# A decoder layer on one core: the second block of each gate/up pair comes only by adding transfers, and the next pair's first product moves ahead of product 7

## The chip, the core and the metric

The kernel runs on one core of a Trainium2 chip. TensorE (PE) multiplies, VectorE (DVE) and ScalarE (ACT) work on tiles, GpSimd (POOL) and SyncE (SP) here mainly start transfers. The metric is the device time of one execution in microseconds, as the median of several runs. A profile shows one further execution in detail.

## The reference, cut to what matters

```python
def _swiglu(x, w_gate, w_up, w_down):
    return (jax.nn.silu(x @ w_gate) * (x @ w_up)) @ w_down
...
h = _layer_norm(ALPHA * h + 0.5 * _swiglu(h, ffn1_w_gate[l], ffn1_w_up[l], ffn1_w_down[l]), ln1_g[l], ln1_b[l])
mix = _mixer(h, positions, w_in[l], ...)          # two attention branches, gates, output projection
h = _layer_norm(ALPHA * h + mix, ln2_g[l], ln2_b[l])
h = _layer_norm(ALPHA * h + 0.5 * _swiglu(h, ffn2_w_gate[l], ffn2_w_up[l], ffn2_w_down[l]), ln3_g[l], ln3_b[l])
```

There are 256 rows of 2048 values, the hidden width of each FFN is 5632, and everything is float32. The change touches the two products with `w_gate` and `w_up` of both FFNs, called the gate/up stage.

## The kernel before

**Products in float32.** A weight tile of 128x1024 (two k-tiles of 128 rows by 512 columns) is read from memory as it is ("raw", "sraw") and split into a high part, cast by ACT (`split`, L154), and the remainder, which DVE computes (L155). Both go into a ring of six slot pairs, "wring". One product of a tile then takes three matmuls (`triple`, L208 to L210: high by high, low by high, high by low).

**Gate/up.** Its columns form 22 chunks of 512 columns, gate and up interleaved. `project` does the first two in the ordinary way. The other 20 go as ten pairs through `Hybrid.group`. A pair has 16 k-tiles of each of two chunks. Of these, k-tiles 0 to 3 and 4 to 7 of the first chunk and of the second form four blocks of weights, "11", "21" (first chunk) and "12", "22" (second), each of two tiles, s0 and s1. The two by two arrangement of blocks is multiplied with the two halves of the rows by seven products instead of eight ("sevenths": 1 to 7 in a scheme like Strassen's). A seventh takes 12 matmuls for its two tiles. The k-tiles that are left, two per step, go as plain steps of 12 matmuls: "p" for the first chunk, "q" for the second. A pair is *wide* when k-tiles 8 and 9 take part in the seven products as a third, half-size tile s2 ("eraw", 128x512): then a seventh has 15 matmuls and there are six plain steps, three for each chunk, instead of eight.

The weights of a seventh are sums of blocks. They are formed in place: DVE adds block 12 to 11 for product 5, 22 to that for product 6, 21 to that for product 4 (L430). For product 7 the sum 12 + 22 is made by a transfer from memory that adds to what lies in the buffer, issued on POOL's queue (L432, `accum_op`).

Products build up in PSUM banks named X, Y, Z, W. Products 1, 6 and 7 share X, products 5 and 3 share Z. ACT copies a bank to "snap" where its value between two products is needed (`after`, L387, L388), and a later matmul into that bank waits for the copy.

**What sets the order.** In each pair, a string gives it, a digit for a product and p or q for a plain step:

```python
            elif wide:
                order = "15pp6p72q4q3q"
            elif seeded:
                order = "15pp6p7p2q4q3qq"
            else:
                order = "1p5p6p7p2q4q3qq"
```

Pairs 2 to 9 of an FFN are wide, the first and the last are not. Each tile of the string becomes a `unit` of three parts, load, prep (sums and split) and now (matmuls); a planner (`look(3, 4)`) starts the loads and preps some units ahead of the matmuls, so the engines' orders are fixed when the program is built. Every engine and queue works its instructions off in that order. FFN2 loads three blocks of its first pair early, under the norm before it: 11, 12 and 22.

Names in the rows: "sraw" are block tiles, "raw" tiles of plain steps, "xs" and "x" or "h" the row operands, "gus", "sg", "hb" the parts of silu times up. POOL's queue also carries the writes of the result towards the down stage ("hT").

## Time and profile before

| | |
|---|---|
| median of 3 runs | 1966.58 us (1965.83 to 1967.08) |
| profiled execution | span 1963.9 us |
| around the span, against the median | 2.7 us |
| PE, DVE, ACT, POOL busy | 1952.0, 1779.9, 1251.5, 312.1 us |
| bytes moved | 488.86 MB, mean 249 GB/s |
| adding transfers of 512 KB | 40, median 7.5 us from issue to landing |

The span is the time from the first to the last recorded instruction of the core. Busy time counts what an engine executes, not the issue of transfers or waits on semaphores. FFN1's adding transfers are issued from 48.7 to 411.4 us of the span, FFN2's from 1316.9 to 1680.2 us; FFN1's down stage and the mixer lie between, FFN2's down stage behind. In rows of a timeline the first number is the start in us, the second the duration, and brackets hold the idle time before, with what ended it.

### The profile page before, as it was taken

The numbers are of one execution on the slowest core, as the hardware profiler recorded it, in microseconds if no ns is written. First come the engines' busy times: TensorE is split into PE (matmuls) and PEld (weight loads), VectorE is DVE, ScalarE is ACT, GpSimd is POOL, SyncE is SP. The second block draws the span as 40 slices with busy tenths as digits, with TensorE's granted clock in tenths as the row PEclk, the third lists the DMA queues.
The fourth block names the chain that finished last, engine by engine and source line by source line (L and its number), as shares of the span: only waits on it lengthen the run. The fifth ranks groups of instructions, "written<-read, shape, count | busy, mean of one in ns | idle before, by whom it ended". The sixth has DMA issues, their size and how long they took to land.

```text
span 1963.9 us, 25802 instructions
## 1 busy us (share of the span) xinstructions
PE 1952.0 (99%) x8763; PEld 1617.7 (82%) x8763; DVE 1779.9 (91%) x2189; ACT 1251.5 (64%) x1640; POOL 312.1 (16%) x536
## 2 busy tenths in 40 slices
PE   9999999999999999999999999999999999999998
PEld 7888888888888898888788888888888888888886
DVE  7999999999998879988987777789999999999997
ACT  6666766676655566666667655556676666665662
POOL 0112111122100010102241530001211112210000
PEclk9999999999999999999999999999999999999999
DMA  8978888878776667767685798587888878787773
GB/s 314 289 225 262 270 260 249 257 233 300 272 235 222 210 216 258 239 223 252 211 254 195 237 305 271 201 264 254 252 269 263 250 240 277 241 318 236 277 232 124
DMA packets 150228, 488.86 MB, mean 249 GB/s; under 512 B 21792, under 2 KB 22096, under 8 KB 150096
## 3 DMA queue, kind: packets, MB, share of 16 engines
q1 hardware_dynamic: 119232, 401.00, 59.7%
q0 software_dynamic: 30720, 86.09, 16.8%
q8 instruction: 68, 1.11, 0.2%
q14 instruction: 64, 0.52, 0.1%
q10 hardware_dynamic: 144, 0.13, 0.0%
HBM read 456.73 MB, written 30.41 MB: 248 GB/s over the span
## 4 chain that ended last, share of the span: by engine, by line
PE 95%; DVE 2%; DMA 1%; issue 1%; ACT 0%; POOL 0%; SPq 0%; DVEq 0%; ACTq 0%; POOLq 0%
PE mm L208 30%; PE mm L210 30%; PE mm L209 30%; DVE wring L155 1%; PE tr L208 1%; PE tr L210 1%; PE tr L209 1%; PE tr L673 0%; DMA turned<-turn 0%; ACT wring L154 0%; DMA sraw<-in_wdk_dram 0%; DVE sraw L430 0%; PE tr L1376 0%; PE tr L1304 0%; PE tr L1378 0%
## 5 line engine op out<-in xcount | busy, mean ns | idle before, releaser
L154 ACT CAST wring<-raw 128x1024 fp32r<-128x1024 f32 (+2 forms) x468 | 482.7, 1035 | 323.5 <-PE mm L210 237.6
L155 DVE TENSOR_TENSOR wring<-raw,wring 128x1024 fp32r<-128x1024 f32 (+2 forms) x468 | 557.0, 1198 | 95.6 <-ACT wring L154 93.5
L154 ACT CAST wring<-sraw 128x1024 fp32r<-128x1024 f32 x436 | 453.1, 1052 | 201.7 <-DVE sraw L430 83.6
L155 DVE TENSOR_TENSOR wring<-sraw,wring 128x1024 fp32r<-128x1024 f32 x436 | 520.3, 1218 | 20.6 <-ACT wring L154 17.8
L208 PE MATMUL mm<-wring,h 128*128 128x512 f32 (+2 forms) x1248 | 480.9, 385 | 0.1
L210 PE MATMUL mm<-wring,h 128*128 128x512 f32 (+2 forms) x1248 | 480.3, 385 | 0.0
L209 PE MATMUL mm<-wring,h 128*128 128x512 f32 (+2 forms) x1248 | 479.9, 385 | 0.0
L208 PE MATMUL mm<-wring,xs 128*128 128x512 f32 x776 | 302.2, 389 | 0.5 <-ACT snap L387 0.5
L209 PE MATMUL mm<-wring,xs 128*128 128x512 f32 x776 | 302.1, 389 | 0.0
L210 PE MATMUL mm<-wring,xs 128*128 128x512 f32 x776 | 301.9, 389 | 0.0
L210 PEld LDWEIGHTS mm<-wring,h 128*128 128x128 f32 x1248 | 234.4, 188 | 47.0 <-DVE h L155 0.7
L208 PEld LDWEIGHTS mm<-wring,h 128*128 128x128 f32 x1248 | 234.4, 188 | 46.7 <-ACT h L154 0.6
L209 PEld LDWEIGHTS mm<-wring,h 128*128 128x128 f32 x1248 | 234.4, 188 | 46.1
L430 DVE TENSOR_TENSOR sraw<-sraw,sraw 128x1024 f32<-128x1024 f32 x168 | 199.1, 1217 | 2.0 <-DMA sraw<-in_wdk_dram 1.6
L208 PEld LDWEIGHTS mm<-wring,xs 128*128 128x128 f32 x776 | 145.6, 188 | 31.0 <-ACT snap L387 0.9
L209 PEld LDWEIGHTS mm<-wring,xs 128*128 128x128 f32 x776 | 145.7, 188 | 30.5 <-DVE wring L155 0.3
L210 PEld LDWEIGHTS mm<-wring,xs 128*128 128x128 f32 x776 | 145.7, 188 | 30.2
L719 POOL DMA_DIRECT2D hT<-blocks x176 | 96.8, 563 | 368.3 <-DVE blocks L717 367.2
L209 PE MATMUL mm<-wring,x 128*128 128x512 f32 x336 | 130.9, 390 | 0.2 <-DVE wring L155 0.2
L208 PE MATMUL mm<-wring,x 128*128 128x512 f32 x336 | 130.1, 390 | 0.8 <-ACT wring L154 0.8
L210 PE MATMUL mm<-wring,x 128*128 128x512 f32 x336 | 130.7, 389 | 0.0
L432 POOL DMA_DIRECT2D sraw<-in_gu_dram x40 | 35.6, 892 | 371.4 <-DVE sraw L430 334.5
(328 smaller groups left out, 2292.4 us busy)
## 6 DMA issues: line engine op xcount, KB each, us to landing
sraw<-in_gu_dram SPq DMA_DIRECT2D x160, 512.0 KB, 5.2
raw<-in_gu_dram SPq DMA_DIRECT2D x158, 512.0 KB, 5.0
raw<-in_dn_dram SPq DMA_DIRECT2D x140, 512.0 KB, 4.7
sraw<-in_gu_dram POOLq DMA_DIRECT2D x40, 512.0 KB, 7.5
sraw<-in_dn_dram SPq DMA_DIRECT2D x36, 512.0 KB, 5.4
eraw<-in_gu_dram SPq DMA_DIRECT2D x64, 256.0 KB, 5.8
raw<-in_w_out_dram SPq DMA_DIRECT2D x32, 512.0 KB, 4.3
hraw<-hT POOLq DMA_DIRECT2D x56, 256.0 KB, 5.9
```

What stands on the lines that cost most here:

```text
L154: cast[0] = S.copy(hi, src)
L155: lows[0] = V.tensor_tensor(out=lo, in0=src, in1=hi.bitcast(F32), op=ALU.subtract)
L208: PE.matmul(o, xh, wh, start=first, stop=False, skip_group_check=again)
L209: PE.matmul(o, xh, wl, start=False, stop=False, skip_group_check=again)
L210: PE.matmul(o, xl, wh, start=False, stop=last, skip_group_check=again)
L430: last = V.tensor_tensor(out=R[src][i], in0=R[src][i], in1=R[add[1]][i], op=ALU.add)
L432: nc.gpsimd.dma_start(R["12"][s], source("22", s), accum_op=ALU.add)
L719: nc.gpsimd.dma_start(to.rearrange("(g r) (i f) -> i r g f", g=4, i=4)[i], t[32 * i:32 * (i + 1), :].rearrange("r (g f) -> r g f", g=4))
```

## The change

All ten pairs are wide, and one order holds for all: the letter n in it stands for the *next* pair's product 1, which a pair after the first then leaves out at its own start. Block 12 is no longer loaded by itself. It is added from memory onto block 11 for product 5, as soon as product 1 has split 11, and onto block 22 for product 7, once product 6's DVE sum has read 22. Product 3, which now comes ahead of 6 and 7, uses 22 as loaded. The buffers of block 11 are two sets, which successive pairs swap. Bank Z comes from another pool of PSUM banks ("tr" instead of "mm"). FFN2's early loads are 11, 22, 21. The mixer's use of the class (`small`) keeps its way.

```diff
+    ORDERS = {(False, False): "1pp5p36np27q4qqq", (True, False): "1p5p36np27q4qq",
+              (False, True): "1pp5p36np27q4qqq", (True, True): "1p5p36np27q4qq"}
+    WIDE = 5
...
-            self.raws = {n: early[n] if n in early else [act_tile([P, 1024], F32, "sraw") for _ in range(2)]
-                         for n in ("11", "12", "22")}
-            self.raws["21"] = [act_tile([P, 1024], F32, "sraw") for _ in range(2)]
+            names = ("11", "12", "22", "21") if small else ("11", "22", "21", "other 11")
...
+        def run(self, groups):
+
+            parts = []
+            for g in groups:
+                parts.append(self.group(*g[:-1]))
+                self.raws["11"], self.raws["other 11"] = self.raws["other 11"], self.raws["11"]
+            for i, (order, emit) in enumerate(parts):
+                groups[i][-1]()
+                for c in order if i == 0 else order[1:]:
+                    if c != "n":
+                        emit(c)
+                    elif i + 1 < len(parts):
+                        parts[i + 1][1]("1")
...
+            added = {}
+            if not small:
+                plan |= {5: (None, "11", None, "Z"), 3: ("22", "22", None, "Z"), 6: (None, "11", ("11", "22"), "X"),
+                         7: (None, "22", None, "X")}
+                added = {1: "11", 6: "22"}
...
-                    banks[n] = mm_bank()
+                    banks[n] = tr_bank() if n == "Z" and not small else mm_bank()
...
-                    if not small and p == 6:
-                        nc.gpsimd.dma_start(R["12"][s], source("22", s), accum_op=ALU.add)
+                    if p == 6 and p in added:
+                        nc.gpsimd.dma_start(R["22"][s], source("12", s), accum_op=ALU.add)
                     pair = [v[:, :tiles * 512] for v in next_pair()]
                     with tc.issue_after(last.ins) if last is not None and not small else nullcontext():
                         split_in_line(not small, *pair, t)
+                    if p == 1 and p in added:
+                        nc.gpsimd.dma_start(R["11"][s], source("12", s), accum_op=ALU.add)
...
-                name, w, j0 = (("11", 2, 0), ("12", 3, 0), ("22", 3, 2))[j // 2]
+                name, w, j0 = (("11", 2, 0), ("22", 3, 2), ("21", 2, 2))[j // 2]
```

In instructions this is 12 matmuls less, 64 adding transfers more on POOL's queue (120 instead of 56), 52 loads less on SP's queue, and 40 adds of 128x1024 less on DVE.

**POOL's queue in FFN1's first pairs.** The rows before, from the first adding transfers on (sraw_465, sraw_466 and eraw_471 are the buffers that the sum for product 7 is made in):

```order
L432 DMA sraw_465<-in_gu_dram 128x1024
L432 DMA sraw_466<-in_gu_dram 128x1024
L719 DMA hT_122<-blocks_632 32x4x128 x4
L719 DMA hT_122<-blocks_653 32x4x128 x4
L432 DMA sraw_465<-in_gu_dram 128x1024
L432 DMA sraw_466<-in_gu_dram 128x1024
L432 DMA eraw_471<-in_gu_dram 128x512
```

And the same place now, where sraw_463, sraw_464 are the first pair's block 11, sraw_465, sraw_466 block 22, and sraw_469, sraw_470 the next pair's block 11:

```order
L458 DMA sraw_463<-in_gu_dram 128x1024
L458 DMA sraw_464<-in_gu_dram 128x1024
L458 DMA eraw_471<-in_gu_dram 128x512
L453 DMA sraw_465<-in_gu_dram 128x1024
L453 DMA sraw_466<-in_gu_dram 128x1024
L453 DMA eraw_471<-in_gu_dram 128x512
L458 DMA sraw_469<-in_gu_dram 128x1024
L749 DMA hT_122<-blocks_614 32x4x128 x4
L458 DMA sraw_470<-in_gu_dram 128x1024
L749 DMA hT_122<-blocks_630 32x4x128 x4
L458 DMA eraw_472<-in_gu_dram 128x512
```

The first pair has gained three additions for product 5 (L458) ahead of those for product 7 (L453), and the next pair's come before the first pair's hT writes are through.

**ACT at the start of FFN1's first pair.** Before, its casts for product 1 (sraw_463, sraw_464), a plain step, and product 5, whose sum DVE has put in the same two buffers, stand in this order:

```order
L154 CAST wring_120<-sraw_463 128x1024
L154 CAST wring_118<-sraw_464 128x1024
L154 CAST wring_116<-raw_477 128x1024
L154 CAST wring_114<-sraw_463 128x1024
L914 ACTIVATE sg_454<-mm_317 128x256
L154 CAST wring_104<-sraw_464 128x1024
L914 ACTIVATE sg_510<-mm_324 128x256
```

Now, with the half-size third tile (eraw_471) in both products:

```order
L154 CAST wring_120<-sraw_463 128x1024
L154 CAST wring_118<-sraw_464 128x1024
L154 CAST wring_116<-eraw_471 128x512
L154 CAST wring_114<-raw_478 128x1024
L944 ACTIVATE sg_454<-mm_317 128x256
L154 CAST wring_104<-sraw_463 128x1024
L154 CAST wring_120<-eraw_471 128x512
L944 ACTIVATE sg_508<-mm_324 128x256
L154 CAST wring_102<-sraw_464 128x1024
```

Product 5's second large tile has moved behind the cast of its half-size tile and a silu.

**ACT around the copy after product 7.** Before, in FFN1's wide pairs, the copy of bank X after 7 (L388 of snap_473) comes behind the casts for product 2 (sraw_469, sraw_470, eraw_472) and for the plain step q (raw_1234):

```order
L154 CAST wring_114<-eraw_471 128x512
L154 CAST wring_104<-sraw_469 128x1024
L387 COPY snap_473<-mm_1112 128x512
L154 CAST wring_102<-sraw_470 128x1024
L154 CAST wring_120<-eraw_472 128x512
L154 CAST wring_118<-raw_1234 128x1024
L388 COPY snap_473<-mm_1112 128x512
```

Now (L409 of snap_473) it comes behind the casts of the third tile of product 7, of q (raw_983, raw_1024) and of product 4's first two tiles (sraw_469, sraw_470):

```order
L154 CAST wring_116<-eraw_471 128x512
L154 CAST wring_114<-raw_983 128x1024
L944 ACTIVATE sg_1020<-mm_675 128x256
L154 CAST wring_104<-sraw_469 128x1024
L154 CAST wring_118<-raw_1024 128x1024
L154 CAST wring_102<-sraw_470 128x1024
L409 COPY snap_473<-mm_655 128x512
L154 CAST wring_120<-eraw_472 128x512
```

Product 2 has moved ahead of 7 (its three casts stand further up), and the plain step q, which writes into the copied bank, follows product 7 directly.

## The prediction

> **What bounds the kernel now.** I read the page's busy times and chain first, then the waits of PE, then windows of single stages, then single instructions.

> ```profile
> span 1963.9 us, 25802 instructions
> PE   1952.0 (99%) x8763; PEld 1617.7 (82%) x8763; DVE 1779.9 (91%) x2189; ACT 1251.5 (64%) x1640; POOL 312.1 (16%) x536
> ...
> PE 95%; DVE 2%; DMA 1%; issue 1%; ACT 0%; POOL 0%; SPq 0%; DVEq 0%; ACTq 0%; POOLq 0%
> ```

> ```profile
> PE tr L869 <- ACT pair L867: 4.1, 1, 4.1
> ...
> PE mm L208 <- ACT wring L154: 0.8, 1, 0.8
> PE mm L208 <- ACT snap L387: 0.5, 1, 0.5
> ```

> ```profile
> core 0: us, PE busy (x) PEld busy (x) DVE busy (x) ACT busy (x) POOL busy (x), PEclk, DMA share, GB/s
> 200.00:250.00 50.00, 50.00 (x222) 41.40 (x221) 49.83 (x56) 32.62 (x42) 7.03 (x11) 1.00 0.86 268
> 600.00:650.00 50.00, 50.00 (x222) 41.42 (x221) 41.86 (x41) 29.83 (x32) 0.00 (x0) 1.00 0.57 183
> 170.00:410.00 240.00, 240.00 (x1060) 198.76 (x1059) 239.01 (x270) 164.15 (x212) 42.17 (x66) 1.00 0.84 258
> 45.00:60.00 15.00, 15.00 (x68) 12.43 (x67) 13.17 (x13) 8.79 (x12) 1.89 (x2) 1.00 1.03 335
> 1300.00:1345.00 45.00, 45.00 (x201) 37.24 (x200) 37.65 (x37) 27.79 (x32) 5.78 (x10) 1.00 0.85 272
> ```

> PE is the bound: 95% of the chain, and hardly a wait in the whole span. The second windows row is the down stage, where VectorE (DVE) is only 84% busy; the first lies in the gate/up pairs, where it is 99.7% busy. Both hold 222 recorded matmuls in 50 us at clock 1.00, so PE's pace isn't set by DVE. DVE merely keeps up. The pace of one matmul, and how soon another engine reacts to it:

> ```profile
> 201.95 0.39 PE L210 MATMUL mm<-wring,xs 128*128 128x512 f32 x1
> 202.18 0.39 PE L208 MATMUL mm<-wring,x 128*128 128x512 f32 x1
> 202.41 0.39 PE L209 MATMUL mm<-wring,x 128*128 128x512 f32 x1
> 202.63 0.39 PE L210 MATMUL mm<-wring,x 128*128 128x512 f32 x1
> ...
> 202.38 1.06 ACT L154 CAST wring<-raw 128x1024 fp32r<-128x1024 f32 x1 [0.99 <-PE mm L210]
> 203.34 1.05 ACT L154 CAST wring<-sraw 128x1024 fp32r<-128x1024 f32 x1
> ```

> Three starts in 202.63 − 201.95 = 0.68 us: 0.227 us a matmul. ACT starts 0.43 us after the start of the matmul that it waits for (202.38 − 201.95), and its casts follow each other by 0.96.

> **Term 1, matmuls.** Four of twenty pairs (first and last of each FFN) become wide: two k-tiles of both chunks, 24 plain matmuls, become seven times three. 4 × 3 × 0.227 = **−2.7 us**, all on PE's path.

> **Term 2, DVE's relief: 0.** A wide pair loses product 5's adds, two of 128x1024 and one of 128x512.

> ```profile
> 45.72 1.22 DVE L155 TENSOR_TENSOR wring<-raw,wring 128x1024 fp32r<-128x1024 f32 x1
> 46.86 2.35 DVE L430 TENSOR_TENSOR sraw<-sraw,sraw 128x1024 f32<-128x1024 f32 x2
> ```

> Two such operations start 1.14 us apart, so 2 × 1.14 plus about half of one is 2.9 us a pair; of 40 us, that makes DVE idle 7%, but no wait of PE goes away. It does give the operand ring a lead that covers small delays.

> **Term 3, FFN1's first pair.** Product 5 took DVE's add of two blocks loaded early; now its operand is made by transfers that start only behind product 1's splits, and only 27 matmuls (product 1 and one plain step, 6 of the chunk before lie between: 33) separate their uses on PE.

> ```profile
> 43.30 2.50 DVE L155 TENSOR_TENSOR wring<-sraw,wring 128x1024 fp32r<-128x1024 f32 x2 [3.47 <-ACT wring L154]
> ...
> 48.70 2.02 POOL L432 DMA_DIRECT2D sraw<-in_gu_dram  x2 [46.59 <-DVE sraw L430]
> ...
> 49.18 0.39 PE L208 MATMUL mm<-wring,xs 128*128 128x512 f32 x1
> ...
> 61.72 1.05 ACT L154 CAST wring<-sraw 128x1024 fp32r<-128x1024 f32 x1 [1.44 <-DMA sraw<-in_gu_dram]
> ```

> ```profile
> DMA to landing us min/median/max: 5.0/7.1/11.8
> ...
> sraw<-in_gu_dram POOLq DMA_DIRECT2D x2, 512.0 KB, 10.4
> ```

> The second fence is the adding line's summary over the kernel, then its row in 45:60, where the DMA share is 1.03. Those two were issued at 48.7 and about 49.9; the second released ACT at 61.72 (11.8 us), so the median of 10.4 leaves 9.0 for the first. The splits end at 44.5 and 45.8. POOL follows the end of DVE's work by 0.6 (48.70 against 46.86 + 1.18), so after the change the issues stand at 45.1, 46.4 and, for the small tile, 47.1. With 9.0 and 11.8 the first two land at 54.1 and 58.2, the third some 2 later (half of the 4.0 between the earlier two), 60.1. PE wants them at 49.18 + 33 × 0.227 = 56.7, 58.0 and 59.4. ACT casts in order: first large tile, small tile, a silu, second large tile. So the second starts at 60.1 + 0.9 = 61.0, DVE's remainder is ready some 2.3 later at 63.3, and PE wants that at 58.3: late by 5.0. At the median of 7.1 all land by 54.2 and nothing waits. Bounds 0 and 7 (small tile 2 later still). I take **+4.0**, nearest to the row of the same place, a little under because one block less is loaded ahead there.

> [...]

> **Term 4, FFN2's first pair.**

> ```profile
> 1308.42 1.22 DVE L155 TENSOR_TENSOR wring<-sraw,wring 128x1024 fp32r<-128x1024 f32 x1 [1.28 <-ACT wring L154]
> ...
> 1311.84 1.22 DVE L155 TENSOR_TENSOR wring<-sraw,wring 128x1024 fp32r<-128x1024 f32 x1
> ...
> 1318.02 0.39 PE L208 MATMUL mm<-wring,xs 128*128 128x512 f32 x1
> ...
> sraw<-in_gu_dram POOLq DMA_DIRECT2D x2, 512.0 KB, 9.8
> ```

> Issues at 1310.2, 1313.7 and 1314.4; with 9.8 us (the last row, of 1300:1345) the last lands at 1324.2, and by the steps of term 3 the second tile's remainder is ready at 1327.4; PE wants it at 1318.02 + 40 × 0.227 = 1327.1. **+0.5**; bounds 0 and 2.5.

> **Term 5, the bank after product 7.** Plain step q writes on in the bank that ACT copies after 7. Before, product 2 lay between in wide pairs (21 matmuls); now 9 do. Ahead of the copy ACT casts two tiles, the first into the slot that 7's second tile frees, 13 matmuls before q's need.

> ```profile
> 957.83 0.57 ACT L387 COPY snap<-mm 128x512 f32<-128x512 f32 x1
> ...
> 958.45 0.50 PE L208 MATMUL mm<-wring,xs 128*128 128x512 f32 x1 [0.51 <-ACT snap L387]
> ```

> 0.43 + 2 × 0.96 + 0.62 (958.45 − 957.83) = 2.97 against 13 × 0.227 = 2.95: 0.02 a pair, 20 pairs, **+0.5**. Bounds 0 and 4 (0.2 a pair, if a cast comes late by that).

> **Term 6, adding transfers in all later pairs: 0.** Per pair block 12 (1.31 MB) changes from plain loads to transfers into memory that add.

> ```profile
> q1 hardware_dynamic: 15788, 50.77, 61.3%
> q0 software_dynamic: 4128, 11.01, 22.7%
> ```

> In 170:410 that is 1.21% a MB against 2.06%; 6 pairs × 1.31 MB × 0.85 = +7%, so a share of 0.91. Product 7's addition is issued some 11 us ahead of its cast, with about 3 us of ring lead behind it: a landing under 14 us is hidden; the longest row is 11.8. Product 1's next block has its own buffer, and product 5's addition most of 14 tiles, near 30 us. SP loses 52 loads. The hT writes queue behind six additions in POOL's queue, but their reader is about 9 us away. Bounds 0 and 1 us a pair.

> ```profile
> L432 POOL DMA_DIRECT2D sraw<-in_gu_dram x40: 847/894/1023, 48.7 to 1680.2; - x40
> ```

> 64 more issues cost POOL 0.9 us each, on an engine 16% busy. [...]

> **The sum:** −2.7 + 4.0 + 0.5 + 0.5 = +2.3. The profiled execution took its span of 1963.9 plus 2.7 around it, the median 1966.58. So **about 1968.9 us**. This measurement tells 0.2% (3.9 us) from no change: the likeliest is no change.

> **The rivals.**
> - *No stall in the first pairs.* The additions land in about 7 us, as in the median; nothing speaks for it in a window of share 1.03. −2.7 + 0.5: 1964.4, still no change. Chance 0.2.
> - *Slower by the first pairs alone.* FFN1's small tile lands at 62, PE late by 7, FFN2's by 2.5: −2.7 + 9.5 + 0.5 = +7.3, 1973.9. It decides from a joint stall of 6.1 us, that is, additions some 1.6 us later than I took. For it: three additions instead of two, into full queues. Against: fewer plain loads ahead. Chance 0.16.
> - *Slower in every pair.* Landing grows past 14 us at a share of 0.91 or more, or the bank's copy comes late by 0.3: each 0.5 us a pair is 10 us, so about 1977 and up to 1990. Against: 9.8 at a share of 0.85, 10.4 at 1.03. Chance 0.14.
> - *DVE was the pace after all*, and its 2.9 us a pair come back: 20 × 2.9 = 58 us, 1909. The two windows with equal counts speak against it; 0.05, with any smaller gain that I can't see.

> My forecast, stalls of 2 to 6 us in all, has 0.45, its own range 1966 to 1970. Faster 0.05; within 0.2% the forecast and the first rival, 0.64; slower 0.31. The range 1963.5 to 1975 leaves out the fourth rival and most of the third.

> **What would show it.** PE's waits should list one of 2 to 6 us on product 5's wring near 58 us and none above 1 us in later pairs; recorded matmuls fall by about 12; DVE's busy time falls by some 40 us with the time unchanged; additions land in 7 to 10 us. I am wrong if PE waits for snap or wring twenty times, or if PE's pace in 200:250 isn't 222 a 50 us.

## The result: 1980.4 us, slower by 0.7%, and the profile after

| | before | after |
|---|---|---|
| median (lowest to highest) | 1966.68 us (1965.83 to 1967.08) | 1980.41 us (1977.12 to 1982.59) |
| ratio to before, 95% interval | | 1.0071 (1.0057 to 1.0085) |
| profiled execution, span | 1963.9 us | 1980.8 us |

The profiled execution of after is the longest of its four, so its span shows +16.9 us where the medians show +13.7. First the head of its page, then PE's waits and those of its weight loads (PEld): line waited for, total us, times, longest.

```profile
span 1980.8 us, 25910 instructions
PE   1960.7 (99%) x8751; PEld 1617.2 (82%) x8751; DVE 1743.7 (88%) x2161; ACT 1269.4 (64%) x1660; POOL 367.8 (19%) x600
```

```profile
PE tr L208 <- ACT wring L154: 4.7, 2, 4.3
PE tr L899 <- ACT pair L897: 4.1, 1, 4.1
PE tr L209 <- DVE wring L155: 3.3, 3, 1.8
...
PE mm L209 <- DVE wring L155: 0.8, 3, 0.4
```

```profile
PEld mm L208 <- ACT snap L409: 6.5, 20, 0.4
```

The 4.1 us of L899 stood in before too. New are some 8 us of waits for the ring, and twenty of the weight load for the snap copy, which PE's own list doesn't show. Busy time hides the rest: PE is "busy" 8.7 us longer with 12 matmuls fewer. The windows tell why, first before's row, then after's:

```profile
50.00:100.00 50.00, 50.00 (x223) 41.38 (x222) 46.04 (x50) 31.51 (x39) 7.79 (x12) 1.00 0.93 288
```

```profile
50.00:100.00 50.00, 44.98 (x183) 36.03 (x182) 37.59 (x41) 29.77 (x38) 9.76 (x14) 0.93 0.89 260
200.00:250.00 50.00, 50.00 (x221) 41.18 (x220) 45.84 (x52) 34.14 (x44) 14.00 (x22) 1.00 0.89 254
170.00:410.00 240.00, 240.00 (x1054) 197.25 (x1054) 223.22 (x251) 167.52 (x209) 57.41 (x83) 1.00 0.85 253
```

In 50:100 forty matmuls are missing: 5 us were idle, and the granted clock was 0.93 in the mean. In 170:410, with no wait to be seen, six are missing (1054 for 1060): each of the six pairs loses about 0.2 us. DVE there fell from 239.01 to 223.22 us and nothing came of it.

Where did it go? I added up what successive starts of 512-column matmuls stand apart beyond 0.2267 us ("lost" from here on; before loses 0 in all three stages): FFN1's gate/up 10.2 us (8.5 in the first pair, 0.17 in each of ten), the first 160 us of FFN1's down stage 4.7, FFN2 4.3 (2.8 at its first pair, the rest 0.17 a pair). 19.2 less the 2.7 of the matmuls saved is 16.5, against 16.9.

**The first pair.** Timelines of ACT and of PE:

```profile
60.49 0.62 ACT L154 CAST wring<-eraw 128x512 fp32r<-128x512 f32 x1 [5.38 <-DMA eraw<-in_gu_dram]
61.01 0.38 ACT L944 ACTIVATE sg<-mm 128x256 f32<-128x256 f32 x1
61.29 1.03 ACT L154 CAST wring<-sraw 128x1024 fp32r<-128x1024 f32 x1
```

```profile
62.38 0.51 PE L208 MATMUL tr<-wring,xs 128*128 128x512 f32 x1 [4.27 <-ACT wring L154]
63.64 0.79 PE L209 MATMUL tr<-wring,xs 128*128 128x512 f32 x1 [0.76 <-DVE wring L155]
64.23 0.63 PE L210 MATMUL tr<-wring,xs 128*128 128x512 f32 x1
64.66 0.63 PE L208 MATMUL tr<-wring,xs 128*128 128x512 f32 x1
```

ACT sat idle until the third adding transfer had landed, and PE waited 4.27 + 0.76 = 5.0 us. Then the matmuls start 0.43 us apart, not 0.227. Windows of 3.413 us from 59.59 on:

```profile
59.59:63.00 3.41, 0.51 (x1) 0.19 (x1) 1.07 (x2) 2.51 (x4) 0.00 (x0) 1.00 0.98 395
63.00:66.41 3.41, 2.77 (x7) 2.19 (x8) 3.41 (x5) 3.17 (x5) 0.00 (x0) 0.50 0.18 56
66.41:69.83 3.42, 3.42 (x10) 2.65 (x9) 3.42 (x5) 1.00 (x2) 0.00 (x0) 0.50 0.42 143
69.83:73.24 3.41, 3.41 (x17) 2.80 (x16) 3.41 (x4) 2.65 (x4) 2.56 (x3) 1.00 0.52 68
```

The granted clock was half for two windows. A full one holds 3.41 × (1 − 0.227/0.427) = 1.6 us of loss, so 5.0 of waiting cost 8.5.

**The copy after product 7**, in one of the twenty pairs: ACT, then the weight load that it holds, then PE.

```profile
132.79 0.57 ACT L409 COPY snap<-mm 128x512 f32<-128x512 f32 x1
```

```profile
133.41 0.19 PEld L208 LDWEIGHTS mm<-wring,x 128*128 128x128 f32 x1 [0.32 <-ACT snap L409]
```

```profile
133.13 0.39 PE L210 MATMUL mm<-wring,xs 128*128 128x512 f32 x1
133.42 0.50 PE L208 MATMUL mm<-wring,x 128*128 128x512 f32 x1
133.75 0.39 PE L209 MATMUL mm<-wring,x 128*128 128x512 f32 x1
```

The two steps are 0.29 and 0.33 where 0.227 is usual: 0.17 us, with no bracket on the matmul.

**FFN1's down stage**, where nothing was changed:

```profile
592.09 0.80 PE L209 MATMUL tr<-wring,xs 128*128 128x512 f32 x1 [1.82 <-DVE wring L155]
```

Some 0.5 us of small waits, this wait, and 3.41 us at half clock behind it: 4.0 lost. DVE comes to its work late there. The same row of it, the first product for the mixer's angles, in before and after:

```profile
559.42 0.67 DVE L1096 TENSOR_SCALAR ang<-invf,pos 128x32 f32<-128x32 f32 x4
```

```profile
573.77 0.67 DVE L1126 TENSOR_SCALAR ang<-invf,pos 128x32 f32<-128x32 f32 x4
```

The stage's first matmul starts at 453.10 in before and at 462.35 in after, so the row stands 106.32 and 111.42 us behind it: 5.1 us later. DVE has waited 10.4 us since then, against 6.6. Behind its last wait, which ends at 552.69, it works without a gap until PE runs into it.

### The profile page after: what moved, and what is told of

Same layout as the page of the kernel before. It is cut to its first block, busy times and chain, and to the rows that moved or that the text cites. A ratio compares the mean times of both kernels' runs of the same rounds, so it can differ in the third digit from the quotient of the medians.

```text
span 1980.8 us, 25910 instructions
## 1 busy us (share of the span) xinstructions
PE 1960.7 (99%) x8751; PEld 1617.2 (82%) x8751; DVE 1743.7 (88%) x2161; ACT 1269.4 (64%) x1660; POOL 367.8 (19%) x600
## 5 line engine op out<-in xcount | busy, mean ns | idle before, releaser
L154 ACT CAST wring<-raw 128x1024 fp32r<-128x1024 f32 (+2 forms) x460 | 474.1, 1035 | 298.9 <-PE mm L210 211.7
L155 DVE TENSOR_TENSOR wring<-raw,wring 128x1024 fp32r<-128x1024 f32 (+2 forms) x460 | 545.4, 1198 | 111.0 <-ACT wring L154 108.7
L154 ACT CAST wring<-sraw 128x1024 fp32r<-128x1024 f32 x436 | 456.2, 1052 | 175.7 <-PE mm L210 67.4
L155 DVE TENSOR_TENSOR wring<-sraw,wring 128x1024 fp32r<-128x1024 f32 x436 | 524.5, 1217 | 47.8 <-ACT wring L154 43.7
L208 PE MATMUL mm<-wring,h 128*128 128x512 f32 (+2 forms) x1176 | 454.4, 386 | 0.0
L209 PE MATMUL mm<-wring,h 128*128 128x512 f32 (+2 forms) x1176 | 452.4, 385 | 0.4 <-DVE wring L155 0.4
L210 PE MATMUL mm<-wring,h 128*128 128x512 f32 (+2 forms) x1176 | 452.6, 385 | 0.0
L208 PEld LDWEIGHTS mm<-wring,h 128*128 128x128 f32 x1176 | 221.2, 188 | 47.0 <-ACT snap L409 3.3
L209 PEld LDWEIGHTS mm<-wring,h 128*128 128x128 f32 x1176 | 221.1, 188 | 44.1 <-DVE wring L155 1.1
L210 PEld LDWEIGHTS mm<-wring,h 128*128 128x128 f32 x1176 | 221.1, 188 | 43.8 <-DVE h L155 0.9
L209 PE MATMUL mm<-wring,xs 128*128 128x512 f32 x616 | 239.9, 390 | 0.2 <-DVE wring L155 0.2
L208 PE MATMUL mm<-wring,xs 128*128 128x512 f32 x616 | 240.1, 390 | 0.0
L210 PE MATMUL mm<-wring,xs 128*128 128x512 f32 x616 | 239.7, 389 | 0.0
L451 DVE TENSOR_TENSOR sraw<-sraw,sraw 128x1024 f32<-128x1024 f32 x128 | 153.7, 1217 | 1.2 <-DMA sraw<-in_wgm_dram 0.7
L209 PEld LDWEIGHTS mm<-wring,xs 128*128 128x128 f32 x616 | 115.7, 188 | 25.1 <-DVE wring L155 1.0
L210 PEld LDWEIGHTS mm<-wring,xs 128*128 128x128 f32 x616 | 115.6, 188 | 24.1
L208 PEld LDWEIGHTS mm<-wring,xs 128*128 128x128 f32 x616 | 115.6, 188 | 24.1
L453 POOL DMA_DIRECT2D sraw<-in_gu_dram x40 | 35.1, 885 | 435.4 <-DVE sraw L451 410.5
L208 PE MATMUL mm<-wring,x 128*128 128x512 f32 x264 | 103.8, 396 | 0.4 <-ACT wring L154 0.4
L209 PE MATMUL mm<-wring,x 128*128 128x512 f32 x264 | 103.4, 392 | 0.2 <-DVE wring L155 0.2
L210 PE MATMUL mm<-wring,x 128*128 128x512 f32 x264 | 103.3, 391 | 0.0
## 6 DMA issues: line engine op xcount, KB each, us to landing
raw<-in_gu_dram SPq DMA_DIRECT2D x150, 512.0 KB, 6.3
raw<-in_dn_dram SPq DMA_DIRECT2D x140, 512.0 KB, 4.6
sraw<-in_gu_dram SPq DMA_DIRECT2D x120, 512.0 KB, 6.7
sraw<-in_gu_dram POOLq DMA_DIRECT2D x80, 512.0 KB, 7.0
sraw<-in_dn_dram SPq DMA_DIRECT2D x36, 512.0 KB, 5.7
raw<-in_w_out_dram SPq DMA_DIRECT2D x32, 512.0 KB, 4.4
```

The costliest lines, as they stand in the source:

```text
L154: cast[0] = S.copy(hi, src)
L155: lows[0] = V.tensor_tensor(out=lo, in0=src, in1=hi.bitcast(F32), op=ALU.subtract)
L208: PE.matmul(o, xh, wh, start=first, stop=False, skip_group_check=again)
L209: PE.matmul(o, xh, wl, start=False, stop=False, skip_group_check=again)
L210: PE.matmul(o, xl, wh, start=False, stop=last, skip_group_check=again)
L451: last = V.tensor_tensor(out=R[src][i], in0=R[src][i], in1=R[add[1]][i], op=ALU.add)
```

## The experiments

All ratios are to before, timed on the same chip in turns. "Lost" is given as FFN1's gate/up / FFN1's down stage / FFN2 (after: 10.2 / 4.7 / 4.3). My theory was that the loss is these three things, each removable: product 5 too soon in the first pair, the plain step right behind 7, and DVE's shortage in the down stage. The rival: the edits only move waits, because ACT and DVE have no lead there.

**late_five**: the first pair's product 5 two plain steps later, which also puts product 2 ahead of 6.

```diff
-(True, False): "1p5p36np27q4qq"
+(True, False): "1ppp5236n7q4qq"
```

> The changed kernel, but in each FFN's first pair the order is 1ppp5236n7q4qq: three plain steps between products 1 and 5 instead of one, 24 matmuls or 5.4 us more for product 5's adding transfers to land. My theory: the 5.0 us wait at 62 us and the 6.8 us at half clock behind it (3.4 us) go, and some 1.6 us of FFN2's first-pair waits: about 1980.4 - 9 = 1971. At most 1 us of PE wait is left there. Rival, that the added transfers load the DMA engines and slow all pairs: the place of product 5 in one pair of ten changes nothing, 1980. Rival, that the clock falls by itself when all pairs are wide: the wait goes (5 us), the half-clock time stays, 1975.

1980.31 us, 1.0075 (1.0062 to 1.0088): missed. Lost 5.7 / 1.5 / 6.7. The wait at 62 us and its half clock are gone, but the rest of the first pair (not the second pair, as the expectation of first_narrow has it) now loses 4.2, and FFN2's 4.9. ACT there, and POOL, which issues the additions for product 7 (L453):

```profile
76.27 1.05 ACT L154 CAST wring<-sraw 128x1024 fp32r<-128x1024 f32 x1 [1.64 <-DMA sraw<-in_gu_dram]
...
80.94 1.05 ACT L154 CAST wring<-sraw 128x1024 fp32r<-128x1024 f32 x1 [1.67 <-DMA sraw<-in_gu_dram]
```

```profile
70.71 0.96 POOL L453 DMA_DIRECT2D sraw<-in_gu_dram  x1
```

ACT waits in the same way, but for product 7. The additions to its two large tiles, issued at 70.71 and 75.25 once product 6's sums have read block 22, took only 5.5 and 5.6 us to land (76.17 and 80.87). In after, 42 matmuls stand between products 6 and 7: the next pair's product 1, a plain step and product 2. Here only product 1's 15 are left, 3.4 us. So nothing is handed on by product 5: the edit cured that, but took away the work that covered product 7's additions. (The second tile of product 6 waits 0.77 us for DVE, too.)

**four_first**: product 4 between 7 and the plain steps, in all pairs ("...274qqq" for "...27q4qq").

> The changed kernel with the orders' end 7q4qq turned into 74qqq in all pairs: product 4 (15 matmuls) lies between product 7 and the plain step q that writes into the bank copied after 7. My theory: the 20 waits on that copy (0.17 us each, a weight load held up by the ACT snap) go: -3.4 us, about 1977, with the first pair's wait and the mixer's unchanged. Rival: the pairs run slower for another reason (DMA share, transfers landing late), then the time stays at 1980 and the gaps move elsewhere.

1979.23 us, 1.0065 (1.0053 to 1.0078). Lost 6.9 / 6.0 / 1.6. The twenty snap waits are gone and no gate/up pair behind the first loses 0.17: the price of term 5 is shown. The down stage took 1.3 back, and the time fell by less than expected.

**last_narrow**: the last pair as before in width.

```diff
-                 True, p > 1, ask ...
+                 p < KF // 4 - 1, p > 1, ask ...
```

> The changed kernel with each FFN's last pair narrow (order 1pp5p36np27q4qqq): 6 matmuls more (+1.4 us). My theory for the wait of PE at 590 us: DVE enters FFN1's down stage some 4 to 5 us later relative to PE, since a wide last pair leaves it less room for the down stage's operands; DVE is then busy without a gap until PE runs into it (2.3 us of waits, then 3.4 us at half clock, 1.7 us). With a narrow last pair DVE's lag falls under 3 us and the wait goes: -4.0 + 1.4, about 1978. Rival: the wait comes from the late z loads on POOL's queue alone (ACT waited 4.9 us for one), not from DVE's load: then it stays and the time is 1981.8.

1979.28 us, 1.0071 (1.0057 to 1.0085). Lost 10.3 / 2.0 / 3.8: the 590 wait belongs to the wide last pair, but waits that cost 2.0 us appear at 515 to 522 us in its place, and DVE's row of the angles still stands 3.3 us later than in before.

**all_three**: the three edits above together.

> The three edits together (first pair 1ppp5236n74qqq, other wide pairs 1p5p36np274qqq, last pair narrow 1pp5p36np274qqqq). If the parts add: 1980.4 - 9 - 3.4 - 2.6 = 1965 to 1966, PE waits back to the 7 us of the kernel before, no half-clock time in the middle. If one part only moves a wait, 1968 to 1975. If the loss is DMA load or a clock that falls by itself: about 1980.

1984.32 us, 1.0093 (1.0080 to 1.0107): missed by 18 us, the worst kernel of all. Lost 6.1 / 4.0 / 11.2. With late_five's order, FFN2's first pair loses 8.3 us in its products 6, 7 and 4, half clock included (4.9 in late_five). The three remedies don't add; the wait for product 7's additions grows.

**first_narrow**: the first pair of each FFN narrow (`p > 1` for `True`), so that its product 5 has no third tile and more plain steps before it.

> The changed kernel with each FFN's first pair narrow (order 1pp5p36np27q4qqq): 6 matmuls more (+1.4 us); two plain steps instead of one between products 1 and 5, no half-size transfer, and VectorE has about 12 us to spare in a narrow pair against 3 in a wide one. late_five showed that a later product 5 alone only moves the wait into the second pair, so my theory is now that the first pair, where the additions land late, needs both the time and VectorE's room: the 8.5 us lost near 62 us and the 2.8 us lost near 1340 us fall to under 1.5 together: 1980 - 10 + 1.4 = 1971. Rival, that the DMA engines, full from 0 to 90 us of the span, set the end of FFN1's first two pairs: 4 us or more stay lost in FFN1, 1975.

1974.63 us, 1.0048 (1.0035 to 1.0061): 3.6 above what I expected. Lost 3.4 / 3.9 / 1.8. The waits for the additions are gone, 1.6 at 66 us (for the snap copy) and the down stage remain. Two of the four pairs' 0.68 us are given up for this.

**z_late**: ACT's scaling of the residual z in the down stage six steps later and behind a cast, to test whether its wait is what makes DVE late.

> The changed kernel with ACT's scaling of the residual tiles z in FFN1's down stage placed six units later, so that ACT doesn't stand before a late z transfer (4.9 us in the changed kernel's profile) with VectorE behind it. My theory: the 4.0 us lost near 590 us goes, 1980 - 4 = 1976; the rest stays. Rival, that VectorE is short of time in FFN1's down stage whatever ACT does: the wait stays within 1 us, 1979 to 1980.

1980.50 us, 1.0075 (1.0061 to 1.0089). The wait of ACT is gone and PE's 1.83 us for DVE at 591.5 stays. So z is not the cause.

**filled**: 24 small matmuls on zeros ahead of the first pair's second tile of product 5, so that PE isn't idle there.

> The changed kernel with 24 small matmuls on a zero tile (result not read) put ahead of the second tile of product 5 in FFN1's first pair, where PE waited 4.3 us. They take some 4 to 5 us that PE would have waited. My theory, that the half-clock time of 6.8 us behind the wait comes from the wait: no half-clock time near 62 us, 3.4 us won, about 1977. Rival, that the clock falls by itself at this place: it still falls, 1980 or more.

1981.67 us, 1.0080 (1.0066 to 1.0094): missed. The half clock at 62 us is gone once PE isn't idle there. But the added matmuls hold PE for 5.5 us, and PE then waits for the snap:

```profile
70.50 0.50 PE L208 MATMUL tr<-wring,xs 128*128 128x512 f32 x1 [2.43 <-ACT snap L410]
...
71.76 0.43 PE L210 MATMUL tr<-wring,xs 128*128 128x512 f32 x1
71.99 0.62 PE L208 MATMUL tr<-wring,xs 128*128 128x512 f32 x1
```

The half clock follows this wait 1.5 us late.

**mended**: first_narrow, four_first and z_late together.

> First pair narrow (1pp5p36np274qqqq), all later pairs wide with the end 74qqq, and the scaling of z later. If the three parts add: 1980 - 10 + 1.4 - 3.4 - 4 = 1964 to 1966, no more than the kernel before; with VectorE short of time in FFN1's down stage 1968 to 1970; if the DMA engines set the first pairs, 1970 to 1974.

1971.69 us, 1.0029 (1.0018 to 1.0039). Lost 1.6 / 4.9 / 0. FFN2 now takes 0.68 us less than before, the gain of its one additional wide pair. By the number alone it is the expectation's last case, the DMA engines; the trace puts 1.6 in the first pair, a wait for the snap copy, and the most into the down stage.

**setup_late**: only one thing against after, the mixer's setup (positions, sines, masks: about 10 us of DVE, added up over its rows in best), which FFN1's down stage carries, from step 70 to 95.

```diff
-            later(70, setup)
+            later(95, setup)
```

> The changed kernel with the mixer's small preparations (positions, masks, angles; about 5 us of VectorE) moved from step 70 to step 95 after FFN1's gate/up, past the place near 590 us where PE waits for VectorE. z_late left that wait as it was (1.83 us), so ACT's stand before z isn't its cause. My theory now: VectorE is short of time from about 545 to 590 us in FFN1's down stage (no idle there), and enters it some 5 us later than in the kernel before; with 5 us of work taken out the wait and the half-clock time behind it (4.0 us) go: about 1976.5. Rival, that a transfer sets the wait there: it stays, 1980.

1983.13 us, 1.0088 (1.0075 to 1.0101). Lost 9.9 / 0.03 / 3.1. Its windows:

```profile
540.00:600.00 60.00, 60.00 (x266) 49.55 (x265) 56.94 (x60) 35.02 (x38) 4.19 (x8) 1.00 0.68 230
...
655.00:705.00 50.00, 45.67 (x203) 35.96 (x201) 44.27 (x89) 31.81 (x47) 4.63 (x8) 1.00 0.66 213
```

PE is full in 540:600, where it wasn't in after (its row for the same window):

```profile
540.00:600.00 60.00, 57.75 (x246) 46.79 (x245) 56.62 (x76) 32.48 (x36) 5.86 (x11) 0.97 0.65 217
```

That DVE lacked time there is shown; but at 655 to 705 us PE is now idle for 4.3 us behind the moved work, and so nothing is won.

**both_narrow**: the first and last pair of each FFN narrow, everything else as in after.

> The changed kernel with the first and the last pair of each FFN narrow, as in the kernel before: block 12 by additions, product 1 ahead, the end 7q4qqq, but no widening and no matmul saved. By the parts measured: 3.4 us for the 20 copies behind product 7, about 2 us at the first pairs, 2 us in FFN1's down stage: 1973. If the loss hangs on the widening alone: 1967.

1972.92 us, 1.0038 (1.0025 to 1.0051), as expected by the theory that widening is only part of it. Lost 5.6 / 1.2 / 1.4: with no wide pair added, the new order and the transfers alone cost 7 us, by a 2.01 us wait for the snap at 67 us with its half clock, by 0.17 in the pairs behind, and by the down stage.

**best**: first pairs narrow with an order of their own, 7 followed by 4 everywhere, setup at 95.

```diff
-(False, False): "1pp5p36np27q4qqq", ... (True, True): "1p5p36np27q4qq"
+(False, False): "1pp5pp36n274qqqq", ... (True, True): "1p5p36np274qqq"
```

> First pair narrow with a second plain step behind product 5 (1pp5pp36n274qqqq), later pairs wide with the end 74qqq, preparations at step 95. If all waits go, what is left is 6 matmuls less (one wide pair more per FFN than in the kernel before): -1.4 us, 1964.6. If VectorE runs short elsewhere in the down stage: 1966 to 1969. If the first pair still waits for its additions: 1968 to 1972.

1970.71 us, 1.0026 (1.0016 to 1.0035). Lost 0 / 1.5 / 0. Both gate/up stages are clean and 0.68 us shorter than before's; waits of 4.4 us in all at 664 to 693 us, behind the moved setup, cost more than that. In the first pairs two plain steps stand between products 1 and 5 here, and 27 matmuls between 6 and 7, and PE waits for neither.

**gap_setup**: best, with the setup at step 82 and held behind a split, so that DVE does it at 612 to 640 us.

```diff
-            later(95, setup)
+            later(82, setup)
...
+        with tc.issue_after(lows[0].ins):
             V.tensor_copy(pos, pos_i)
```

> The orders of best (first pair narrow with an order of its own, the rest wide with the seventh product last), and the mixer's setup neither where it was (about 545 to 600 us) nor where best has it (655 to 690 us): it is held behind a VectorE split so that it falls near 615 us, where VectorE was busy 5.7 to 6.6 of 10 us in best. Theory (what is left over before in best is only VectorE's shortage around the moved setup): its waits at 664, 669 and 693 us are gone, FFN1's down stage then loses the 1.5 us at 547 us alone, and the time is 1964 to 1967 us. Rival (VectorE has no room for some 14 us of setup anywhere in the down stage, because the splits that follow lose their lead): waits of 1 us or more of the products for a split between 620 and 660 us, and 1969 to 1972 us.

1965.55 us, 0.9998 (0.9989 to 1.0007): level with before, as the theory said, and some 14 us below after. Lost 0 / 1.5 / 0.

```profile
540.00:560.00 20.00, 18.78 (x84) 15.21 (x82) 18.77 (x21) 13.09 (x15) 1.77 (x4) 1.00 0.76 253
...
620.00:660.00 40.00, 40.00 (x178) 33.10 (x178) 39.83 (x60) 26.64 (x29) 0.00 (x0) 1.00 0.65 207
660.00:700.00 40.00, 39.84 (x190) 32.15 (x189) 27.44 (x46) 25.20 (x46) 5.18 (x9) 1.00 0.64 218
```

DVE is full in 620:660 and PE doesn't wait once. One wait is left, 1.22 us for DVE at 548 us, just what the two wide pairs gain (1.4).

## Why the prediction was wrong

The direction's likeliest case, no change at 1968.9, failed; 1980.4 lies outside the range.

- *What bounds the kernel, terms 1, 2 and 6* held. Matmul records fell by 12, and where nothing waits the gain is there: FFN2 in mended and best takes 0.68 us less a wide pair added. DVE fell by 36 us without effect. The DMA share in 170:410 was 0.85 (I said 0.91), POOL's issues took 0.85 us, and in that window the additions landed within their cover:

```profile
sraw<-in_gu_dram POOLq DMA_DIRECT2D x24, 512.0 KB, 7.0
eraw<-in_gu_dram POOLq DMA_DIRECT2D x12, 256.0 KB, 9.1
```

- *Term 3* had the right mechanism and, in its working, the right wait: third addition landed at 60.1 predicted, ACT released at 60.49; the second tile's remainder at 63.3, PE at 63.64; 5.0 us late and 5.0 measured. Two steps failed. I rounded down to 4.0 for the block less that is loaded ahead, though the additions came in 11.1 and 14.4 us. And I priced a wait at its own length: half clock behind it makes it 8.5, beyond the bound of 7.

```profile
sraw<-in_gu_dram POOLq DMA_DIRECT2D x2, 512.0 KB, 11.1
...
eraw<-in_gu_dram POOLq DMA_DIRECT2D x1, 256.0 KB, 14.4
```

- *Term 4*: 2.8 for 0.5, above its bound of 2.5; two waits of 0.4 and 0.8 at 1341 and smaller ones up to 1370. The mechanism is term 3's: ACT was idle for 5.4 us until the third addition landed, 11.5 us after its issue, where I took 9.8. That the later ones come from a ring without lead is likely, not shown.
- *Term 5* was mis-sized: 0.17 a pair for 0.02, 3.4 us for 0.5, inside its bound of 4. I compared the copy's end with the matmul's start; it is the weight load that waits, one step ahead of its matmul. In the rows at 133 us the load, at 133.41, begins while the matmul of 133.13, 0.39 us long, still runs. four_first takes the term away.
- *The step that was missing* is the down stage, which I took as unchanged. In the new order DVE comes there 5.1 us late, and, with hardly any idle time there already before (59.41 of 60 us, in the row below), it can't catch up: 4.7 us. setup_late shows the shortage. The wait near 590 us stands in all seven kernels that have a wide last pair and the setup in its old place, and in none of the three with a narrow one. But the wide last pair is only a part: those three wait near 515 us, and over the ten, DVE's row of the angles stands between 2.4 us (both_narrow, 1.2 lost in the down stage) and 8.1 us late (four_first, 6.0 lost). Which wait of DVE behind the stage's start costs it the 5 us isn't settled; z is excluded. The windows row of before:

```profile
540.00:600.00 60.00, 60.00 (x267) 49.67 (x266) 59.41 (x94) 37.06 (x42) 3.86 (x7) 1.00 0.76 249
```

- *The rivals.* The joint stall of the second (slower by first pairs alone, 0.16) came: 5.0 + 1.2, just past the 6.1 from which it was to decide, and it cost 11.3. My sign for the third, PE waiting for snap twenty times, came true too, at a third of its price. I added neither to the other, though nothing made them exclude each other. One slip in the working changes nothing: the chances listed make 0.65 for no change and 0.30 for slower, not 0.64 and 0.31.

Sum by the measured terms, term 5 without the pair that term 4's 2.8 already holds: −2.7 + 8.5 + 2.8 + 3.2 + 4.7 = +16.5. That is the profiled execution, the slowest of four; the medians differ by 13.7.

## What to carry to other kernels

In a kernel that waits nowhere, a gain of 2.7 us of matmuls lasts only if no new wait arises: look for the next stages in which a feeding engine has no slack, even if the change doesn't touch them, and move their optional work to where that engine is idle (gap_setup: 5 us against best). Price a wait of PE with the half clock that may follow (5.0 us of waiting cost 8.5 in after's first pair), and count a bank's copy against the weight load, not the matmul (0.17 us a pair here). Count the work between issue and use for every late operand, not only for the one that is being cured: late_five gave product 5 its time and took product 7's.

## What the runs showed of the hardware

```profile
583.03:586.44 3.41, 1.59 (x7) 0.87 (x6) 3.41 (x4) 3.06 (x4) 0.00 (x0) 1.00 0.59 177
586.44:589.85 3.41, 3.41 (x10) 2.67 (x9) 3.41 (x6) 0.77 (x1) 0.00 (x0) 0.50 0.80 274
```

```profile
587.33:590.74 3.41, 1.76 (x7) 0.91 (x5) 3.41 (x4) 2.63 (x3) 0.00 (x0) 1.00 0.42 147
590.74:594.15 3.41, 2.62 (x11) 2.17 (x12) 3.41 (x4) 1.26 (x2) 0.00 (x0) 1.00 0.91 294
```

```profile
590.07:593.49 3.42, 1.80 (x8) 1.49 (x9) 3.42 (x4) 2.09 (x3) 0.00 (x0) 1.00 0.81 241
593.49:596.90 3.41, 3.41 (x17) 2.83 (x16) 3.41 (x7) 1.74 (x2) 0.98 (x2) 1.00 0.87 245
```

Twelve such windows at full clock in the FFN stages, in ten of the runs, were followed by half clock, and PE was busy in them for 0 to 1.59 us. The shortest busy times that none followed are 1.70 (setup_late, 694.26), 1.73 (best, 687.04) and the 1.76 above. And a half window with PE busy for 2.77 us (after, 63.00) was followed by one more, one with 3.39 (after, 592.07) was not. So the 1.82 us of idleness that lie in one window in first_narrow cost 1.6 more (an estimate, from the steps of 0.427 in a full half window), and the 1.83 and 1.82 that a border divides in z_late and four_first nothing more. A wait of that length cost either, which may be why the runs of after spread over 5.5 us (before: 1.3), though only one execution of each was profiled.
